# Banded attention: products with the values in float32r with split operands for two heads at a time, while the residual waits in DRAM

## The chip, the core and the metric

The kernel runs on one core of a Trainium2 chip. TensorE (PE in the rows, PEld for its weight loads), VectorE (DVE), ScalarE (ACT), GpSimd (POOL) and the DMA queues each work through a list of instructions of their own, in order, and wait for one another through semaphores. The metric is device time in microseconds of one execution.

## What is computed

The program is two blocks of a network on 512 tokens of width 1024: a recurrent layer and a differential attention layer with their MLPs, then a block that merges a banded attention with a state-space branch, followed by cross attention and an MLP. The change is in the banded attention of the second block: 16 query heads of 64, four key and value heads, blocks of 128 queries that see their own block of keys and its two neighbours, ALiBi, and a sink in the denominator.

```python
def windowed_gqa_sink(q, k, v, sink):
    ...
    s = jnp.einsum('bnqgrd,bnkgd->bngrqk', qb, kw).astype(jnp.float32) * (d ** -0.5) + bias[None]
    sink_f = sink.astype(jnp.float32).reshape(1, 1, kvh, r, 1, 1)
    m = jnp.maximum(jnp.max(s, axis=-1, keepdims=True), sink_f)
    p = jnp.exp(s - m)
    denom = jnp.sum(p, axis=-1, keepdims=True) + jnp.exp(sink_f - m)
    o = jnp.einsum('bngrqk,bnkgd->bnqgrd', (p / denom).astype(v.dtype), vw)
...
    merged = (jax.nn.sigmoid(gate_a) * (attn @ w_attn_branch[i])
              + jax.nn.sigmoid(gate_b) * (ssd @ w_ssd_branch[i]))
    x = x + merged @ w_out[i]
```

## The kernel before

Everything is float32 in value. A large product is made of three float32r products of split operands (`mm3`, lines 457 to 459): an operand is a high half, rounded to float32r by ScalarE, and a low half, the rest, subtracted by VectorE (`split`, lines 465 and 466). Weights come by SP's DMA queue into three `raw` buffers and are split into six `hl` buffers (lines 165 and 167). `feat` gives a projection with features on partitions, `tok` and `tok2` with tokens on partitions; they use the three PSUM buffers `psm`, the attention the five buffers `pss`.

The stage goes through 16 heads `hq`. A projection `gq` (two tiles of `feat`) gives the queries of four heads, so four of them; after heads 3 and 11 `gate_b` makes four tiles of another (`gb`). For a head, `Head.weights(n)` takes query block n: two float32r products over all 128 rows (query and its rest lie in one operand, keys and their rests in `k_hl`) give the scores of two or three key blocks, 256 or 384 columns (line 1476); one VectorE instruction adds the ALiBi term `A` and takes the minimum (1479; scores carry a minus sign); ScalarE takes the exponential with its sum (1481). After block 3 the sink's exponential (1484), the sum (1485) and the reciprocal (1486) follow. `Head.values(n)` multiplies the weights `e` by the reciprocal on VectorE (1494), transposes them on TensorE (1497), copies them out of PSUM on ScalarE (1499) and multiplies with the values in float32, 64 columns of stationary values against 128 queries (1501). Both heads of a pair write into one PSUM bank, which is split into `uk(i)` when the second is done.

The loop calls `values(n)` of head `hq - 2` ahead of `weights(n)` of head `hq`. Behind the stage come the tiles of `ga`, copied into `ta` (1533), which lies in the place of `A`, `e` and `PT` (`wk.phase()`). No hand orders the engines' lists: the framework's scheduler takes instructions in about program order, and what is ready earlier moves ahead, so the projections lie between the heads' steps as far as the buffers let them.

`h` holds the residual. The state-space branch before uses its place, so it waits in DRAM (`hD`, line 1169) and is loaded on GpSimd's queue before this stage (1432); it is next added to by the products with `w_out`, behind the stage.

```python
        if hq < 16:
            heads.append(Head(hq))
        for n in range(4):
            if hq >= 2:
                heads[hq - 2].values(n)
            if hq < 16:
                heads[hq].weights(n)
```

Of the kernel before, what the change touches and what calls it, by code (L numbers as in the profile page):

```python
# [18 lines left out]
P = 128  # L19
S = 512  # L20
D = 1024
NT = 4
# [224 lines left out]
def body(ctx, tc, I, out, dbg=None, stop=None):  # L247
    nc = tc.nc
# [14 lines left out]
    def PS():  # L263
        return ps_s.tile([P, 512], F32, tag="s", name="pss")
# [96 lines left out]
    WT = Weights(nc, raw_p, spl_p, specs, 6, 3)  # L361
# [4 lines left out]
    h = fix.tile([P, NT, D], F32, name="h")  # L366
# [14 lines left out]
    ident = const.tile([P, P], F32, name="ident")  # L381
# [22 lines left out]
    ps = PS()  # L404
# [12 lines left out]
    st = {}  # L417
# [11 lines left out]
    def open_wk(rounded=0):  # L429

        if "wctx" in st:
            st["wctx"].close()
        st["wctx"] = ExitStack()
        wp = st["wctx"].enter_context(tc.tile_pool(name="wp", bufs=1))
        n = 8384 - rounded
        st["wk"] = Work(wp.tile([P, n], F32, name="WK"), n)
        if rounded:
            r = wp.tile([P, rounded], F32R, name="WR")
            return [r[:, i:i + 512] for i in range(0, rounded, 512)]

    def close_b():
# [5 lines left out]
    def uk(k):  # L447
        if k < 4:
            return UAh[:, k], UAl[:, k]
        return st["UBh"][:, k - 4], st["UBl"][:, k - 4]  # L450
# [10 lines left out]
    def split(dst, src, scale=None):  # L461

        hi, lo = dst
        if scale is None:
            nc.scalar.activation(out=hi, in_=src, func=AF.Copy)  # L465
            nc.vector.tensor_tensor(out=lo, in0=src, in1=hi.bitcast(F32), op=ALU.subtract)  # L466
        else:
            nc.scalar.activation(out=hi, in_=src, func=AF.Copy, scale=scale)  # L468
            nc.vector.scalar_tensor_tensor(out=lo, in0=src, scalar=scale, in1=hi.bitcast(F32), op0=ALU.mult, op1=ALU.subtract)
# [115 lines left out]
    def tok(w, src, evac, n_k=8, tiles=NT):  # L585

        for t in range(0, tiles, 2):
            ps = PM()
            for j in range(2):
                o = ps[:, j * 256:(j + 1) * 256]  # L590
                tk = slice((t + j) * P, (t + j + 1) * P)
                for k in range(n_k):
                    xh, xl = src(k)
                    mm3(o, (xh[:, tk], xl[:, tk]), w[k], k == 0, k == n_k - 1)
            evac(slice(t, t + 2), ps.rearrange("p (a b) -> p a b", a=2))
# [164 lines left out]
    o = 0  # L760
# [6 lines left out]
    ps = PS()  # L767
    nc.tensor.transpose(ps[:, :n_rows], ROWS, ident[:n_rows, :n_rows])
    nc.scalar.activation(out=COL, in_=ps[:, :n_rows], func=AF.Copy)
    y = st["ev"].tile([P, D], F32, tag="y", name="y")  # L770
# [496 lines left out]
    class Group:  # L1267


        def __init__(s, g):  # L1270
            s.g, s.hs = g, 4 * g
# [157 lines left out]
        G[g].third()  # L1429
    ssd_out_group(7)  # L1430
    for t in range(NT):
        nc.gpsimd.dma_start(h[:, t], hD[t * P:(t + 1) * P, :])
    for t in range(NT):
        dump("ssd", acc[:, t], t)
    st["ctx"].close()
    open_b()
# [2 lines left out]
        return  # L1439


    KP = open_wk(4096)
    wk = st["wk"]
    k_hl = [KP[0:4], KP[4:8]]

    def gk_evac(n, ps):

# [5 lines left out]
                nc.vector.tensor_tensor(out=kl[r1], in0=ps[r], in1=kh[r].bitcast(F32), op=ALU.subtract)  # L1453

    feat(WT.get("gk"), xk, gk_evac)
    v = st["GP"].rearrange("p (t n) -> p t n", t=NT)
    tok(WT.get("gv"), xk, lambda t, ps: nc.scalar.activation(out=v[:, t], in_=ps, func=AF.Copy))
    pos = {}

    class Head:  # L1460
        def __init__(s, hq):
            s.hq, s.i, s.p, s.kv = hq, hq // 2, hq % 2, hq // 4
            s.A = wk.get("A", 384, 2)
            nc.vector.tensor_scalar(out=s.A, in0=band, scalar1=float(2.0 ** (-0.5 * (hq + 1))), scalar2=None, op0=ALU.mult)
            s.mn = sm.tile([P, 16], F32, tag="mg", name="mg")
            s.es = []

        def weights(s, n):

            hq, mn = s.hq, s.mn  # L1470
            lo, hi = max(0, n - 1), min(4, n + 2)
            wd = (hi - lo) * P
            bo = (lo - n + 1) * P
            ps = PS()
            for x in range(2):
                nc.tensor.matmul(ps[:, :wd], uk(s.i)[s.p][:, n * P:(n + 1) * P], k_hl[x][s.kv][:, lo * P:hi * P],  # L1476
                                 start=x == 0, stop=x == 1)
            e = wk.get(f"e{wd}", wd, 4)
            nc.vector.tensor_tensor_reduce(out=e, in0=ps[:, :wd], in1=s.A[:, bo:bo + wd], scale=1.0,
                                           scalar=nsink[:, hq:hq + 1], op0=ALU.add, op1=ALU.min, accum_out=mn[:, n:n + 1])  # L1480
            nc.scalar.activation(out=e, in_=e, func=AF.Exp, scale=-1.0, bias=mn[:, n:n + 1], accum_out=mn[:, 4 + n:5 + n])
            s.es.append((e, lo, hi))
            if n == 3:
                nc.scalar.activation(out=mn[:, 8:12], in_=mn[:, 0:4], func=AF.Exp, bias=sink[:, hq:hq + 1])
                nc.vector.tensor_tensor(out=mn[:, 8:12], in0=mn[:, 8:12], in1=mn[:, 4:8], op=ALU.add)
                nc.vector.reciprocal(out=mn[:, 12:16], in_=mn[:, 8:12])

        def values(s, n):
            if s.p == 0 and n == 0:
                pos[s.i] = PS()  # L1490
            po, r0 = pos[s.i], slice(64 * s.p, 64 * s.p + 64)
            e, lo, hi = s.es[n]
            wd = (hi - lo) * P
            nc.vector.tensor_scalar(out=e, in0=e, scalar1=s.mn[:, 12 + n:13 + n], scalar2=None, op0=ALU.mult)
            pt = PS()
            for j in range(hi - lo):
                nc.tensor.transpose(pt[:, j * P:(j + 1) * P], e[:, j * P:(j + 1) * P], ident)  # L1497
            PT = wk.get("PT", 384, 2)
            nc.scalar.activation(out=PT[:, :wd], in_=pt[:, :wd], func=AF.Copy)
            for j in range(hi - lo):  # L1500
                nc.tensor.matmul(po[r0, n * P:(n + 1) * P], v[:, lo + j, s.kv * 64:(s.kv + 1) * 64], PT[:, j * P:(j + 1) * P],  # L1501
                                 start=j == 0, stop=j == hi - lo - 1)
            if s.p == 1 and n == 3:
                split(uk(s.i), po)

    def gate_b(u):
        def gb_evac(t, ps):
# [4 lines left out]

        tok2(WT.get(f"gb{u}"), xk, gb_evac)

    heads = []
    for hq in range(18):
        u = hq // 4
        if hq % 4 == 0 and u < 4:
            feat(WT.get(f"gq{u}"), xk, lambda n, ps: split_q(2 * u + n, ps))
        if hq < 16:  # L1520
            heads.append(Head(hq))
        for n in range(4):
            if hq >= 2:
                heads[hq - 2].values(n)
            if hq < 16:
                heads[hq].weights(n)
        if hq % 8 == 3 and hq < 16:
            gate_b(u)
    wk.phase()
    ta = wk.get("ta", 4096).rearrange("p (t n) -> p t n", t=NT)  # L1530
    for u in range(2):
        tok2(WT.get(f"ga{u}"), xk,
             lambda t, ps: nc.scalar.activation(out=ta[:, t, u * 512:(u + 1) * 512], in_=ps, func=AF.Tanh, scale=0.5))
# [165 lines left out]
```

## Time and profile before

| | |
|---|---|
| median of 3 runs | 2580.79 us (2578.79 to 2582.44) |
| profiled execution, its own time | 2581.83 us |
| its span | 2580.1 us |
| PE, PEld busy | 2504.9 us (97%), 2088.2 us (81%) |
| DVE, ACT, POOL busy | 1714.5, 1220.2, 183.5 us |
| mean granted clock of TensorE | 0.989 |

The span is the time from the first to the last instruction; the rest of an execution's time lies around it. A matmul's length in a row is from its start to the modelled end of its pipeline, so neighbours overlap: what one costs TensorE is read from start to start. An fp32 product stands as two rows. The granted clock is 1.00 at 2.4 GHz and 0.50 at 1.2 GHz.

### The profile page before, as it was taken

What the parts mean: (1) busy time and instruction counts of PE and PEld (TensorE: products, weight loads), DVE (VectorE), ACT (ScalarE), POOL (GpSimd) and SP (SyncE); (2) the same over time, 40 slices, a digit from 0 to 9 for tenths busy, and PEclk for the clock granted to TensorE, in tenths of its full rate; (3) what the DMA queues carried; (4) which work ended last, traced back from release to release, by engine and by line L of the source; (5) the groups of instructions that cost most, each with busy time, mean ns of one, the idle gap of its engine ahead of it and who ended that gap; (6) DMA issues with size and microseconds to landing.
All of it is one profiled execution on the core that took longest, in us unless ns stands there. A gap on an engine that the chain in (4) does not pass through costs nothing. (4 is left out here: it accounts for less than half of the span.)

```text
span 2580.1 us, 33650 instructions
## 1 busy us (share of the span) xinstructions
PE 2504.9 (97%) x12848; PEld 2088.2 (81%) x12848; DVE 1714.5 (66%) x3048; ACT 1220.2 (47%) x2181; POOL 183.5 (7%) x199
## 2 busy tenths in 40 slices
PE   8999999999999989999999999998999999999998
PEld 7888888778888768877888788787887789878877
DVE  5566567775566657577477788887555466487674
ACT  6333345443476554444356554563455436444342
POOL 1100220000201030000121100010000000100000
PEclk9999999999999989999999999998999999999999
DMA  5521235333232133453334333352221233243441
GB/s 175 162 66 61 87 115 169 125 108 129 82 96 89 63 97 113 140 179 98 102 109 125 106 104 109 104 148 77 73 67 40 84 113 123 82 147 104 141 139 58
DMA packets 202001, 278.11 MB, mean 108 GB/s; under 512 B 10800, under 2 KB 127776, under 8 KB 201840
## 3 DMA queue, kind: packets, MB, share of 16 engines
q1 hardware_dynamic: 190352, 236.29, 29.4%
q0 software_dynamic: 10192, 34.96, 5.0%
q10 hardware_dynamic: 1296, 4.72, 0.5%
q8 instruction: 101, 1.65, 0.3%
q14 instruction: 60, 0.49, 0.1%
HBM read 271.56 MB, written 9.61 MB: 109 GB/s over the span
## 5 line engine op out<-in xcount | busy, mean ns | idle before, releaser
L458 PE MATMUL psm<-XTl,hl 128*128 128x512 f32 (+1 forms) x1400 | 537.3, 384 | 7.8 <-DVE XTl L466 7.8
L457 PE MATMUL psm<-XTh,hl 128*128 128x512 f32 (+1 forms) x1400 | 534.5, 382 | 5.9 <-ACT XTh L465 5.1
L459 PE MATMUL psm<-XTh,hl 128*128 128x512 f32 (+1 forms) x1400 | 533.3, 382 | 0.0
L165 ACT ACTIVATE hl<-raw 128x1024 fp32r<-128x1024 f32 x303 | 319.3, 1056 | 313.9 <-PE psm L459 132.6
L167 DVE TENSOR_TENSOR hl<-raw,hl 128x1024 fp32r<-128x1024 f32 x287 | 352.7, 1233 | 149.0 <-ACT hl L165 147.9
L458 PEld LDWEIGHTS psm<-XTl,hl 128*128 128x128 f32 x1400 | 266.3, 190 | 56.9 <-DVE XTl L466 8.6
L457 PEld LDWEIGHTS psm<-XTh,hl 128*128 128x128 f32 x1400 | 265.9, 190 | 55.7 <-ACT XTh L465 6.1
L459 PEld LDWEIGHTS psm<-XTh,hl 128*128 128x128 f32 x1400 | 266.3, 190 | 48.5
L457 PE MATMUL psm<-hl,XTh 128*128 128x512 f32 (+1 forms) x640 | 231.1, 362 | 4.4 <-ACT XTh L465 3.3
L458 PE MATMUL psm<-hl,XTh 128*128 128x512 f32 (+1 forms) x640 | 229.9, 359 | 0.1
L459 PE MATMUL psm<-hl,XTl 128*128 128x512 f32 (+1 forms) x640 | 229.1, 358 | 0.0
L457 PE MATMUL psm<-hl,UAh 128*128 128x512 f32 x368 | 148.6, 405 | 4.9 <-DVE ACC L625 1.5
L458 PE MATMUL psm<-hl,UAh 128*128 128x512 f32 x368 | 144.9, 395 | 0.0
L459 PE MATMUL psm<-hl,UAl 128*128 128x512 f32 x368 | 143.7, 396 | 0.0
L457 PEld LDWEIGHTS psm<-hl,XTh 128*128 128x128 f32 x640 | 122.3, 191 | 21.8 <-ACT XTh L465 3.7
L458 PEld LDWEIGHTS psm<-hl,XTh 128*128 128x128 f32 x640 | 122.2, 191 | 16.6 <-issue 0.5
L459 PEld LDWEIGHTS psm<-hl,XTl 128*128 128x128 f32 x640 | 122.3, 191 | 15.9 <-issue 0.5
L671 ACT ACTIVATE WK<-psm 128x512 f32<-128x512 f32 x66 | 39.5, 598 | 160.8 <-PE psm L459 160.8
L457 PE MATMUL psm<-hl,UBh 128*128 128x512 f32 (+1 forms) x240 | 93.5, 391 | 1.1 <-ACT UBh L468 0.8
L459 PE MATMUL psm<-hl,UBl 128*128 128x512 f32 (+1 forms) x248 | 94.3, 388 | 0.0
L1257 DVE SCALAR_TENSOR_TENSOR WS<-psm,CW,WS 128x511 f32<-128x511 f32 (+1 forms) x120 | 87.5, 740 | 8.7 <-ACT WS L1253 8.4
L458 PE MATMUL psm<-hl,UBh 128*128 128x512 f32 (+1 forms) x240 | 92.2, 386 | 0.0
(481 smaller groups left out, 4839.2 us busy)
## 6 DMA issues: line engine op xcount, KB each, us to landing
raw<-in_mlp_w_down_dram SPq DMA_DIRECT2D x76, 512.0 KB, 3.3
raw<-in_mlp_w_up_dram SPq DMA_DIRECT2D x64, 512.0 KB, 3.9
raw<-in_w_in_dram SPq DMA_DIRECT2D x60, 512.0 KB, 3.7
raw<-in_w_down_dram SPq DMA_DIRECT2D x38, 512.0 KB, 3.9
WS<-aD POOLq DMA_DIRECT2D x32, 512.0 KB, 5.9
raw<-in_w_up_dram SPq DMA_DIRECT2D x32, 512.0 KB, 3.7
raw<-in_w_in_dram SPq DMA_DIRECT2D x33, 256.0 KB, 3.2
raw<-in_a_w_in_dram SPq DMA_DIRECT2D x16, 512.0 KB, 4.9
```

Of the source, the lines that this page charges most:

```text
L165: s.nc.scalar.activation(out=h, in_=r, func=AF.Copy)
L167: eng.tensor_tensor(out=l, in0=r, in1=h.bitcast(F32), op=ALU.subtract)
L457: nc.tensor.matmul(ps, a[0], b[0], start=first, stop=False, skip_group_check=partial)
L458: nc.tensor.matmul(ps, a[0], b[1], start=False, stop=False, skip_group_check=partial)
L459: nc.tensor.matmul(ps, a[1], b[0], start=False, stop=last, skip_group_check=partial)
L671: nc.scalar.activation(out=rl, in_=ps, func=AF.Relu)
L1257: nc.vector.scalar_tensor_tensor(out=dst[:, o0:o1], in0=ps[:, o0 + d:o1 + d], scalar=cw(j), in1=dst[:, o0:o1], op0=ALU.mult, op1=ALU.add)
```

## The change

- The stage goes through eight pairs of heads. `values(n)` of pair i - 1 is called ahead of `weights(n)` of pair i.
- The values are split (`gv_evac`): for each key block and value head, 64 columns of high and 64 of low halves lie side by side in `v_hl`, one stationary operand of 128 columns.
- The weights of both heads are transposed side by side, two key blocks (512 columns) to a chunk, and split into `PT` high and low (two buffers). A query block has one or two chunks. Each key block takes two float32r products of 256 columns, with the high and with the low half of `PT` (line 1534 of the new program).
- The output has the high half's part on 64 partitions and the low half's on the other 64, heads swapped over; a copy on ScalarE (1540) and an addition on VectorE (1541) of 64 rows by 256 columns join them into `y`, for each head after blocks 1 and 3. `y`, now in SBUF, is split into `uk(i)`.
- The multiplication with the reciprocal moves from VectorE to GpSimd (1498).
- `e` and `y` lie in the place of `h`, `A` in that of `GP`; `k_hl`, `PT` and `v_hl` fill a rounded tile `WR` of 8192 words. The load of `h` moves behind the stage. `ta` comes from a work area opened anew, whose place `WR` had.

```diff
-    for t in range(NT):
-        nc.gpsimd.dma_start(h[:, t], hD[t * P:(t + 1) * P, :])
...
-    KP = open_wk(4096)
-    wk = st["wk"]
+    KP = open_wk(8192)
+
+    hw, gw = Work(h.rearrange("p t d -> p (t d)"), 4096), Work(st["GP"], 1024)
     k_hl = [KP[0:4], KP[4:8]]
+    WR = st["WR"]
+    PTs = [WR[:, 4096 + 1024 * i:5120 + 1024 * i].rearrange("p (x n) -> p x n", x=2) for i in range(2)]
+    v_hl = WR[:, 6144:8192].rearrange("p (t k n) -> p t k n", t=NT, k=4)
...
-    tok(WT.get("gv"), xk, lambda t, ps: nc.scalar.activation(out=v[:, t], in_=ps, func=AF.Copy))
+    def gv_evac(t, ps):
+
+        hi, lo = (v_hl[:, t, :, 64 * x:64 * x + 64] for x in range(2))
+        ps = ps.rearrange("p a (k n) -> p a k n", k=4)
+        nc.scalar.activation(out=hi, in_=ps, func=AF.Copy)
+        nc.vector.tensor_tensor(out=lo, in0=ps, in1=hi.bitcast(F32), op=ALU.subtract)
+
+    tok(WT.get("gv"), xk, gv_evac)
...
+        def scale(s, n):
+            e, lo, hi = s.es[n]
+            nc.gpsimd.tensor_scalar(out=e, in0=e, scalar1=s.mn[:, 12 + n:13 + n], scalar2=None, op0=ALU.mult)
+
+    class Pair:
+
+
+        def __init__(s, i):
+            s.i, s.kv = i, i // 2
+            s.heads = [Head(2 * i), Head(2 * i + 1)]
+            s.y = hw.get("yv", 512, 2).rearrange("p (n q) -> p n q", n=4)
+
+        def weights(s, n):
+            for x in s.heads:
+                x.weights(n)
+
         def values(s, n):
...
-            nc.vector.tensor_scalar(out=e, in0=e, scalar1=s.mn[:, 12 + n:13 + n], scalar2=None, op0=ALU.mult)
-            pt = PS()
-            for j in range(hi - lo):
-                nc.tensor.transpose(pt[:, j * P:(j + 1) * P], e[:, j * P:(j + 1) * P], ident)
-            PT = wk.get("PT", 384, 2)
-            nc.scalar.activation(out=PT[:, :wd], in_=pt[:, :wd], func=AF.Copy)
-            for j in range(hi - lo):
-                nc.tensor.matmul(po[r0, n * P:(n + 1) * P], v[:, lo + j, s.kv * 64:(s.kv + 1) * 64], PT[:, j * P:(j + 1) * P],
-                                 start=j == 0, stop=j == hi - lo - 1)
-            if s.p == 1 and n == 3:
-                split(uk(s.i), po)
+            lo, hi = s.heads[0].es[n][1:]
+            for x in s.heads:
+                x.scale(n)
+            if n % 2 == 0:
+                s.po = PS()
+            o = s.po[:, n % 2 * 256:n % 2 * 256 + 256]
+            for j0 in range(lo, hi, 2):
+                js = range(j0, min(j0 + 2, hi))
+                w = 256 * len(js)
+                pt = PS()
+                for j in js:
+                    for x in s.heads:
+                        c = (j - j0) * 256 + x.p * P
+                        nc.tensor.transpose(pt[:, c:c + P], x.es[n][0][:, (j - lo) * P:(j - lo + 1) * P], ident)
+                st["pt"] = st.get("pt", 0) + 1
+                PT = PTs[st["pt"] % 2]
+                split((PT[:, 0, :w], PT[:, 1, :w]), pt[:, :w])
+                for j in js:
+                    c = slice((j - j0) * 256, (j - j0) * 256 + 256)
+                    for x in range(2):
+                        nc.tensor.matmul(o, v_hl[:, j, s.kv], PT[:, x, c], start=j == lo and x == 0, stop=j == hi - 1 and x == 1)
+            if n % 2 == 1:
+                po = s.po.rearrange("p (n x q) -> p n x q", n=2, x=2)
+                y = s.y[:, n - 1:n + 1]
+                for x in range(2):
+                    r, r1 = slice(64 * x, 64 * x + 64), slice(64 - 64 * x, 128 - 64 * x)
+                    nc.scalar.activation(out=y[r], in_=po[r1, :, x], func=AF.Copy)
+                    nc.vector.tensor_tensor(out=y[r], in0=po[r, :, x], in1=y[r], op=ALU.add)
+            if n == 3:
+                split(uk(s.i), s.y.rearrange("p n q -> p (n q)"))
...
-    for hq in range(18):
-        u = hq // 4
-        if hq % 4 == 0 and u < 4:
+    for i in range(9):
+        u = i // 2
+        if i % 2 == 0 and u < 4:
             feat(WT.get(f"gq{u}"), xk, lambda n, ps: split_q(2 * u + n, ps))
...
-            if hq >= 2:
-                heads[hq - 2].values(n)
-            if hq < 16:
-                heads[hq].weights(n)
+            if i >= 1:
+                pairs[i - 1].values(n)
+            if i < 8:
+                pairs[i].weights(n)
...
-    wk.phase()
+    open_wk(4096)
+    wk = st["wk"]
     ta = wk.get("ta", 4096).rearrange("p (t n) -> p t n", t=NT)
+    for t in range(NT):
+        nc.gpsimd.dma_start(h[:, t], hD[t * P:(t + 1) * P, :])
```

TensorE, late in the stage, before the change. L1476 are score products, L1497 transpositions, L1501 value products; `pss` is PSUM, `WR` the keys, `UB` the queries, `WK` holds `e` and the transposed weights, `GP` the values.

```order
L1476 MATMUL pss<-WR,UBh 128x256 x2
L1497 MATMUL pss<-ident,WK 128x128 x3
L1476 MATMUL pss<-WR,UBh 128x384 x2
L1497 MATMUL pss<-ident,WK 128x128 x3
L1476 MATMUL pss<-WR,UBh 128x384 x2
L1501 MATMUL pss<-WK,GP 64x128 x3
L1497 MATMUL pss<-ident,WK 128x128 x2
L1476 MATMUL pss<-WR,UBh 128x256 x2
L1501 MATMUL pss<-WK,GP 64x128 x3
L1497 MATMUL pss<-ident,WK 128x128 x2
```

Transpositions and value products are those of head `hq - 2`, score products those of head `hq`; a whole head lies between a head's last score products and its first transposition.

TensorE at the same place after the change: L1484 are score products, L1527 transpositions (out of `h`, where `e` lies), L1534 value products (`WR` holds values and `PT`).

```order
L1527 MATMUL pss<-ident,h 128x128 x4
L1534 MATMUL pss<-WR 128x256
L1484 MATMUL pss<-WR,UBh 128x256 x2
L1484 MATMUL pss<-WR,UBl 128x256 x2
L1534 MATMUL pss<-WR 128x256 x4
L1527 MATMUL pss<-ident,h 128x128 x4
L1534 MATMUL pss<-WR 128x256
L1484 MATMUL pss<-WR,UBh 128x256 x2
L1484 MATMUL pss<-WR,UBl 128x256 x2
L1527 MATMUL pss<-ident,h 128x128 x4
```

The two rows of 256-column score products in the middle are the last of pair p + 1; four value products of pair p's block 3 follow, then the first four transpositions of pair p + 1 itself. From there to the end of the stage no projection stands in the list; behind its last value products the products of `ga` go on.

GpSimd after the change, the eight multiplies of one pair; the number behind `mg` tells the head. Before, GpSimd's list has nothing in this stage.

```order
L1498 TENSOR_SCALAR h_78<-h_78,mg_14366 128x256
L1498 TENSOR_SCALAR h_78<-h_78,mg_14366 128x384 x2
L1498 TENSOR_SCALAR h_78<-h_78,mg_14366 128x256
L1498 TENSOR_SCALAR h_78<-h_78,mg_14368 128x256
L1498 TENSOR_SCALAR h_78<-h_78,mg_14368 128x384 x2
L1498 TENSOR_SCALAR h_78<-h_78,mg_14368 128x256
```

All four blocks of a pair's first head stand ahead of the second head's.

## Rows read from the trace of the kernel before

**Rows 1.** Windows: length; PE, PEld, DVE, ACT, POOL busy (instructions); PEclk; DMA share; GB/s.

```profile
1841.00:1976.70 135.70, 135.70 (x729) 109.68 (x727) 75.31 (x190) 69.90 (x164) 0.00 (x0) 1.00 0.21 63
1976.70:2013.20 36.50, 35.97 (x245) 26.98 (x244) 24.03 (x89) 26.85 (x84) 0.00 (x0) 1.00 0.01 1
2013.20:2036.30 23.10, 23.09 (x117) 17.50 (x117) 6.09 (x8) 9.28 (x15) 0.00 (x0) 1.00 0.29 92
```

**Rows 2.** Groups by line, 1841 to 2036 us: busy us, mean ns | idle before.

```profile
L1501 PE MATMUL pss<-WK,GP 128*64 128x128 f32 x319 | 43.5, 281 | 0.0
...
L1479 DVE CUSTOM_DVE_ANT_0 WK<-pss,WK,nsink 128x384 f32<-128x384 f32 x32 | 19.6, 616 | 19.9 <-PE pss L1476 19.7
L1481 ACT ACTIVATE WK<-WK,mg 128x384 f32<-128x384 f32 x32 | 19.6, 612 | 8.3 <-DVE mg L1479 8.2
...
L1481 ACT ACTIVATE WK<-WK,mg 128x256 f32<-128x256 f32 x32 | 16.0, 501 | 1.9 <-DVE mg L1479 1.8
L1479 DVE CUSTOM_DVE_ANT_0 WK<-pss,WK,nsink 128x256 f32<-128x256 f32 x32 | 15.4, 480 | 18.9 <-PE pss L1476 18.8
...
L1494 DVE TENSOR_SCALAR WK<-WK,mg 128x384 f32<-128x384 f32 x32 | 11.9, 415 | 0.0
L1494 DVE TENSOR_SCALAR WK<-WK,mg 128x256 f32<-128x256 f32 x32 | 11.2, 350 | 0.4
...
L1464 DVE TENSOR_SCALAR WK<-band 128x384 f32<-128x384 f32 x14 | 5.0, 359 | 0.4
...
L466 DVE TENSOR_TENSOR UAl<-pss,UAh 128x512 fp32r<-128x512 f32 x4 | 2.8, 692 | 3.7 <-ACT UAh L465 3.6
...
L465 ACT ACTIVATE UAh<-pss 128x512 fp32r<-128x512 f32 x4 | 2.4, 598 | 5.3 <-PE pss L1501 5.3
```

**Rows 3.** Timeline from 1932.2 us: start, length, engine, line, instructions.

```profile
1932.23 0.30 PEld L1476 LDWEIGHTS pss<-WR,UAl 128*128 128x128 f32 x2
1932.25 0.49 PE L1476 MATMUL pss<-WR,UAl 128*128 128x256 f32 x2
1932.47 0.35 PEld L1497 LDWEIGHTS pss<-ident,WK 128*128 128x128 f32 x3
1932.58 0.49 PE L1497 MATMUL pss<-ident,WK 128*128 128x128 f32 x3
...
1932.80 0.30 PEld L1476 LDWEIGHTS pss<-WR,UAl 128*128 128x128 f32 x2
1932.80 0.47 DVE L1479 CUSTOM_DVE_ANT_0 WK<-pss,WK,nsink 128x256 f32<-128x256 f32 x1
...
1933.16 0.49 ACT L1499 ACTIVATE WK<-pss 128x384 f32<-128x384 f32 x1 [0.18 <-PE pss L1497]
```

**Rows 4.** Timeline: the last steps of a head's weights.

```profile
1928.92 0.16 DVE L1485 TENSOR_TENSOR mg<-mg 128x4 f32<-128x4 f32 x1
1929.12 0.18 DVE L1486 RECIPROCAL mg<-mg 128x4 f32<-128x4 f32 x1
```

**Rows 5.** A subtraction of 256 columns out of PSUM (line 1382).

```profile
L1382 DVE TENSOR_TENSOR WS<-pss,WS x32: 402/416/425, 1405.5 to 1787.3; 128x256 f32<-128x256 f32 x32
```

**Rows 6.** GpSimd's groups by line, whole span.

```profile
L634 POOL TENSOR_TENSOR WK<-ACC,GP 128x512 f32<-128x512 f32 x32 | 43.6, 1376 | 362.5 <-DVE ACC L625 349.0 <-DVE h L637 12.4 <-DVE rr L484 1.0
L167 POOL TENSOR_TENSOR hl<-raw,hl 128x1024 fp32r<-128x1024 f32 x16 | 41.9, 2636 | 411.5 <-ACT hl L165 411.5
```

**Rows 7.** Timeline of TensorE: two idle times before 1782.5 and 1790.7 us.

```profile
1782.52 1.97 PE L1381 MATMUL pss<-WS 128*128 128x64 f32 x8 [2.42 <-DVE WS L1382]
...
1790.67 1.94 PE L1394 MATMUL pss<-ident,h 128*128 128x128 f32 x8 [3.35 <-DVE h L1392]
```

**Rows 8.** Windows at half the clock.

```profile
1782.00:1790.60 8.60, 3.94 (x16) 3.56 (x16) 5.90 (x19) 1.93 (x8) 1.01 (x1) 0.50 0.13 50
...
1793.10:1799.00 5.90, 5.83 (x14) 4.58 (x15) 1.41 (x2) 0.60 (x2) 0.35 (x1) 0.50 0.54 181
```

**Rows 9.** Additions into the residual `h` after the stage (line 625).

```profile
L625 DVE TENSOR_TENSOR h<-psm,h x16: 673/688/692, 2098.2 to 2144.2; 128x512 f32<-128x512 f32 x16
```

More of the change, by code (lines that the diff above doesn't have):

```diff
@@ L437, in open_wk @@
         if rounded:
-            r = wp.tile([P, rounded], F32R, name="WR")
+            r = st["WR"] = wp.tile([P, rounded], F32R, name="WR")
             return [r[:, i:i + 512] for i in range(0, rounded, 512)]
@@ L1455, in body @@
     feat(WT.get("gk"), xk, gk_evac)
-    v = st["GP"].rearrange("p (t n) -> p t n", t=NT)
-    tok(WT.get("gv"), xk, lambda t, ps: nc.scalar.activation(out=v[:, t], in_=ps, func=AF.Copy))
-    pos = {}
+    def gv_evac(t, ps):
[4 more added lines that the diff above has]
+    tok(WT.get("gv"), xk, gv_evac)
     class Head:
@@ L1462, in __init__ @@
             s.hq, s.i, s.p, s.kv = hq, hq // 2, hq % 2, hq // 4
-            s.A = wk.get("A", 384, 2)
+            s.A = gw.get("A", 384, 2)
             nc.vector.tensor_scalar(out=s.A, in0=band, scalar1=float(2.0 ** (-0.5 * (hq + 1))), scalar2=None, op0=ALU.mult)
@@ L1477, in weights @@
                                  start=x == 0, stop=x == 1)
-            e = wk.get(f"e{wd}", wd, 4)
+            e = hw.get(f"e{wd}", wd, 4)
             nc.vector.tensor_tensor_reduce(out=e, in0=ps[:, :wd], in1=s.A[:, bo:bo + wd], scale=1.0,
@@ L1486, in weights @@
                 nc.vector.reciprocal(out=mn[:, 12:16], in_=mn[:, 8:12])
-        def values(s, n):
[L1489 to L1493, printed above, removed]
-            nc.vector.tensor_scalar(out=e, in0=e, scalar1=s.mn[:, 12 + n:13 + n], scalar2=None, op0=ALU.mult)
-            pt = PS()
-            for j in range(hi - lo):
-                nc.tensor.transpose(pt[:, j * P:(j + 1) * P], e[:, j * P:(j + 1) * P], ident)
-            PT = wk.get("PT", 384, 2)
-            nc.scalar.activation(out=PT[:, :wd], in_=pt[:, :wd], func=AF.Copy)
-            for j in range(hi - lo):
-                nc.tensor.matmul(po[r0, n * P:(n + 1) * P], v[:, lo + j, s.kv * 64:(s.kv + 1) * 64], PT[:, j * P:(j + 1) * P],
-                                 start=j == 0, stop=j == hi - lo - 1)
-            if s.p == 1 and n == 3:
-                split(uk(s.i), po)
+        def scale(s, n):
+            e, lo, hi = s.es[n]
+            nc.gpsimd.tensor_scalar(out=e, in0=e, scalar1=s.mn[:, 12 + n:13 + n], scalar2=None, op0=ALU.mult)
@@ L1513, in gate_b @@
         tok2(WT.get(f"gb{u}"), xk, gb_evac)
-    heads = []
-    for hq in range(18):
-        u = hq // 4
-        if hq % 4 == 0 and u < 4:
+    pairs = []
+    for i in range(9):
+        u = i // 2
+        if i % 2 == 0 and u < 4:
             feat(WT.get(f"gq{u}"), xk, lambda n, ps: split_q(2 * u + n, ps))
-        if hq < 16:
-            heads.append(Head(hq))
+        if i < 8:
+            pairs.append(Pair(i))
         for n in range(4):
-            if hq >= 2:
-                heads[hq - 2].values(n)
-            if hq < 16:
-                heads[hq].weights(n)
-        if hq % 8 == 3 and hq < 16:
+            if i >= 1:
+                pairs[i - 1].values(n)
+            if i < 8:
+                pairs[i].weights(n)
+        if i % 4 == 1 and i < 8:
             gate_b(u)
-    wk.phase()
+    open_wk(4096)
+    wk = st["wk"]
     ta = wk.get("ta", 4096).rearrange("p (t n) -> p t n", t=NT)
+    for t in range(NT):
+        nc.gpsimd.dma_start(h[:, t], hD[t * P:(t + 1) * P, :])
     for u in range(2):
```

## Prediction

> **What bounds the kernel now.** Read first the windows of the stage. From the first score product to the last value product it takes 195.3 us in three stretches [rows 1]: 135.7 us with projections between the attention's products, 36.5 us without any, 23.1 us with products of gate `ga` between the last heads'. See that TensorE is busy for all of each at full clock, while DVE is busy 105.4 us and ACT 106.0 us in the sum. So here TensorE's work is the time, and latency costs nothing. Then read the groups by line: the 160 fp32 products with the values (two trace rows each) hold TensorE 43.5 us [rows 2], 0.272 us each with the entry and exit of their bursts. Then read the timeline for what a float32r product of 256 columns takes: two issue in 1932.23 to 1932.47, 0.12 us each; three transpositions in 1932.47 to 1932.80, 0.11 each [rows 3].
>
> **The change part by part.** *Value products.* 160 fp32 products of 0.272 us become 160 float32r ones (8 pairs x 10 blocks x 2 halves), 256 columns wide, at 0.12. With latency hidden that is 160 x 0.152 = 24.3 us less. Bounds of the new price: 0.12 [rows 3] and, if they issued no faster than now, 0.272 [rows 2]. I take 0.12, the row with type and width in common.
>
> *Where they stand* (counted in TensorE's list of instructions). Projections are the only work that can fill TensorE's waits, and the same 406 products stand in the first stretch before and after; but before they accompany 78 of the 160 value products, 82 of the 160 transpositions and 74 score products, now 44, 50 and 54. A pair now holds `e` from its scores to its values with no head between, and the list runs out of projections earlier. So:
>
> - First stretch: less 78 x 0.272 = 21.2, less 32 x 0.11 = 3.5, less 10 score products of 256 columns at 0.12 and 10 of 384 at an estimated 0.18 (1.5 times as wide) = 3.0, plus 44 x 0.12 = 5.3: 135.7 - 22.4 = 113.3 us. TensorE stays the bound there, since DVE's 75 and ACT's 70 us [rows 1] leave room.
> - Third stretch: the 18 value products (4.9) and 10 transpositions (1.1) leave, 23.1 - 6.0 = 17.1; its copies into `ta` now wait until everything in `WR` is done, and three tiles of `ga` hold all `psm` buffers till then. One copy of 512 columns (0.60 [rows 2]), the half result ahead of it on ACT and hand-overs: 1.2. Together 18.3 us.
> - Second stretch: 116 value products, 110 transpositions and 74 score products, and no projection. TensorE's part is small: a pair takes 20 x 0.11 + 20 x 0.12 + 8 x 0.12 + 8 x 0.18 = 7.0 us. The time is the loop from pair to pair.
>
> *The loop, first half,* from the last score products of pair p+1 to its first transposition. Score product to DVE 0.55 (1932.25 to 1932.80 [rows 3]); two reductions of 256, 0.96 [rows 2]; then on DVE, ahead of the sums, the low half of pair p's last chunk 0.69 and two `A` tiles 0.72 [rows 2]; sum 0.16 and reciprocal 0.18 [rows 4]: 3.3 us. Then POOL: it has all four multiplies of head 0 ahead of head 1's, and the second transposition is head 1's, so five multiplies (three of 256, two of 384) stand in the way. Before, values ran two heads behind scores and this lay under the head between.
>
> *Price of a multiply on GpSimd.* The trace has none with one input. Lower bound: DVE's own 0.350 and 0.415 [rows 2], 1.9 us for the five. Upper: GpSimd's two-input rows, 1376 ns for 512 and 2636 for 1024 columns [rows 6], that is 0.116 + 2.46 ns a column, 0.75 and 1.06: 4.4 us. I take the middle, 3.1, since one input is less than two but the engine is GpSimd. With 0.2 of hand-overs the first half is 6.6 us.
>
> The Trainium skill, GPSIMD Engine Reference, Engine selection, calls one-input elementwise work on GpSimd "roughly line-rate" and sends elementwise tiles to VectorE. By its rate the price would lie at the lower bound and the sum 7 us lower; no run here shows it yet.
>
> *Second half,* from there to the next last score products, a zigzag in which each engine's list makes it wait for the other: four transpositions to ACT 0.7 (0.58 for three [rows 3], one more 0.11), high half 0.60, low half 0.69, reduction 256 0.48, two exponentials 1.00, high half 0.60, low halves 0.69 and 0.42, reduction 384 0.62, two exponentials 1.22, high half 0.60, low half 0.69, sum of the halves 0.42, reduction 384 0.62, low half 0.42, last products 0.3 [rows 2, 5]: 10.1 us. (256-column subtractions and the 64-row sum are priced by line 1382.)
>
> So 16.7 us a pair, with TensorE at work for 7.0. The stretch holds the rest of pair 2 (half of the zigzag and one first half, 11.7), four full loops (66.8) and pair 7's values without scores, six chunks of high and low half, about 8: 86.5 us in place of 36.5.
>
> *Clock.* TensorE idles over 3 us in every first half. In the trace it was granted 0.50 (1.2 of 2.4 GHz) from 1782 on, after idle times of 2.42 and 3.35 us [rows 7], through sparse work and through 5.9 us of dense products at the end [rows 8]. Half rate adds between 1.5 us (transpositions, score and last products that lie on the loop) and 7.0 us (all its work) to a pair. Weighing it as present about half the time, nearer the lower end, I take 1.2 a pair, 7 us in all, and nothing for the restart.
>
> *Edits at nothing.* The `h` load: four issues leave POOL at 1792, where nothing follows, and come behind the last multiply; the first use was at 2098.2 [rows 9], 62 us behind the stage. The `mem` load on POOL, now ahead of pair 7's multiplies, waits only for the last reductions, which these wait for too. Two low halves of the values (0.69 each) lie under projections. SP's list is unchanged.
>
> *Sum.* 113.3 + 86.5 + 18.3 = 218.1, plus 7 = 225 for 195.3: 29.8 more. The profiled execution took 2581.83, so 2611.6 there; it lies 1.0 above the median of the runs, 2580.79. **Forecast: 2611 us.**
>
> The Trainium skill, SBUF — State Buffer, has VectorE operations with two SBUF inputs and GpSimd operations lock each other out of a shared port pair. The split of a finished pair (inputs now both in SBUF) falls among the multiplies; by the rule it would add at most one 0.69 a pair, 4 us.
>
> **Rivals.**
> - *The loop overlaps better than the lists say* and only DVE's own time counts in the second stretch: per pair 6.0 us for values (four low halves of 0.69, two of 0.42, four sums of 0.42, the pair's split 0.69) and 5.8 for scores (four reductions of 0.48, four of 0.62, 0.72 for `A`, 0.68 for sums and reciprocals). 5.8 pairs of values (116 of 20) and 4.6 of scores (74 of 16) make 61.5: 113.3 + 61.5 + 18.3 = 193.1, 2.2 under before: 2579 us, not slower. It decides below a loop of 11.0 us, where the second stretch comes to 63.7. For it: DVE and ACT were busy only 24 and 27 of 36.5 us [rows 1]. Against it: each step above waits for a result.
> - *TensorE stays the bound throughout:* 24.3 us less, 2556. It needs projections in the second stretch, and the list has none.
> - *Half clock throughout:* 4 us a pair and 3 at the restart, 26 in place of 7: 2630. For it the long idle times; against it, dense runs of several us in each loop.
> - *Cheap multiplies at full clock:* 1.2 a pair less, no clock term: 2598; with a loop of 14 us, 2589.
>
> **How the numbers follow.** Forecast 0.65 (2598 to 2622), half clock 0.15, cheap and short 0.12, DVE's time 0.05, TensorE's bound 0.03. The range 2590 to 2632 leaves out the last two and the tails. A measurement tells 0.2%, 5.2 us, from no change. Slower: the first three, 0.92. DVE's time, 2.2 us, falls within: same 0.05. TensorE's bound alone is faster: 0.03.
>
> **What would show it.** Windows: first stretch near 113 us with TensorE full; then 85 to 95 us with TensorE under half busy and one wait for POOL per pair of over 3 us. Groups: float32r products without bursts' gaps, multiplies on POOL of 0.4 to 1.0 us. PEclk at half for part of the second stretch. Wrong: a second stretch under 64 us, or TensorE full in it; multiplies outside their bounds; time moved outside the stage.

## Result and profile after the change

| | before | after |
|---|---|---|
| median of 4 runs each, same chip | 2581.61 us (2578.79 to 2582.87) | 2616.94 us (2616.21 to 2618.18) |
| profiled execution, its own time | 2581.83 us | 2618.18 us |
| its span | 2580.1 us | 2616.1 us |
| PE, PEld busy | 2504.9, 2088.2 us | 2498.3, 2092.0 us |
| DVE, ACT, POOL busy | 1714.5, 1220.2, 183.5 us | 1735.8, 1233.0, 258.8 us |
| mean granted clock | 0.989 | 0.978 |

The ratio is 1.0139 (95% interval 1.0121 to 1.0156): slower, 36 us by the spans. The first addition into `h` behind the stage came at 2098.2 us before [rows 9] and comes at 2134.6 now, 36.4 later; the first score product comes at 1843.2 for 1841.3. So the loss lies in the stage: it takes 34.3 us more. Of the other 2 us, 1.6 are there at the first product of line 1381, long ahead of the changed code: 1401.9 us before, 1403.5 here. It starts at 1405.5 in e4_before_scale_gpsimd, which differs from the kernel before only later, so this is scatter between executions.

```profile
L625 DVE TENSOR_TENSOR h<-psm,h x16: 672/688/692, 2134.6 to 2180.6; 128x512 f32<-128x512 f32 x16
```

Windows of the kernel after, with the columns of [rows 1]. The first boundary is where the projections run out and 44 value products are done, as counted in the prediction; the second is the last value product; the third row holds the 70 products of `ga` that stood inside the stage before.

```profile
1843.18:1955.00 111.82, 111.82 (x557) 94.70 (x556) 63.62 (x133) 57.02 (x121) 30.07 (x24) 1.00 0.26 76
1955.00:2055.50 100.50, 58.30 (x300) 48.90 (x298) 55.52 (x164) 52.67 (x146) 46.34 (x44) 0.75 0.04 14
2055.50:2072.80 17.30, 16.21 (x72) 13.27 (x72) 6.17 (x7) 8.20 (x12) 0.53 (x1) 1.00 0.60 198
```

To be read against [rows 1]: TensorE full in the first stretch, 58% busy in the second, where the granted clock is 0.75 and no engine comes near its length. For whom TensorE waited in the second stretch (1955 to 2056 us; engine line waited for: us in total, times, longest us):

```profile
PE pss L1527 <- POOL h L1498: 26.9, 10, 4.4
PE pss L1534 <- ACT WR L465: 9.5, 12, 1.4
PE pss L1534 <- DVE WR L466: 5.4, 6, 1.1
```

The same view of the whole stage before has 0.5 us in all. One loop of the second stretch, from the timeline (start, length, engine, line, instructions, [idle before]):

```profile
1981.35 0.18 DVE L1494 RECIPROCAL mg<-mg 128x4 f32<-128x4 f32 x1
...
1981.72 9.02 POOL L1498 TENSOR_SCALAR h<-h,mg 128x256 f32<-128x256 f32 x8 [10.23 <-DVE mg L1493]
...
1982.70 0.33 PE L1527 MATMUL pss<-ident,h 128*128 128x128 f32 x1 [1.31 <-POOL h L1498]
...
1987.45 0.90 PE L1527 MATMUL pss<-ident,h 128*128 128x128 f32 x3 [4.42 <-POOL h L1498]
1988.45 0.60 ACT L465 ACTIVATE WR<-pss 128x512 fp32r<-128x512 f32 x1 [4.66 <-PE pss L1527]
1989.08 0.69 DVE L466 TENSOR_TENSOR WR<-pss,WR 128x512 fp32r<-128x512 f32 x1 [4.51 <-ACT WR L465]
...
1998.54 0.45 PE L1484 MATMUL pss<-WR,UBl 128*128 128x256 f32 x2
...
2001.14 0.18 DVE L1494 RECIPROCAL mg<-mg 128x4 f32<-128x4 f32 x1
...
2001.51 0.92 POOL L1498 TENSOR_SCALAR h<-h,mg 128x256 f32<-128x256 f32 x1 [10.77 <-DVE mg L1493]
```

GpSimd starts its eight multiplies 0.2 us behind the end of the first head's reciprocal (shown; the second head's starts 0.28 later). The second head's first transposition waits until 1987.45, five multiplies and 5.73 us later, and ScalarE and VectorE stand idle for over 4.5 us behind it. The zigzag (the blocks in which TensorE, ScalarE and VectorE wait for each other in turn) to the pair's last scores takes 1987.45 to 1998.54, sums and reciprocals 2.97 more, and the next multiplies start at 2001.51.

What a multiply and a value product take (groups by line of the stage, columns of [rows 2]):

```profile
L1498 POOL TENSOR_SCALAR h<-h,mg 128x384 f32<-128x384 f32 x32 | 42.8, 1346 | 0.0
L1534 PE MATMUL pss<-WR 128*128 128x256 f32 x160 | 40.3, 339 | 15.3 <-ACT WR L465 9.5 <-DVE WR L466 5.4
...
L1498 POOL TENSOR_SCALAR h<-h,mg 128x256 f32<-128x256 f32 x32 | 32.0, 1004 | 172.2 <-ACT mg L1492 80.2 <-DVE mg L1494 31.8 <-DVE mg L1493 31.6
```

From start to start a value product takes 0.120 us where the granted clock is 1.00 (median of 128) and 0.214 where it is 0.50 (median of 32), against 0.272 before. Five of them at half the clock, 1993.53 to 1994.60:

```profile
1993.53 1.27 PE L1534 MATMUL pss<-WR 128*128 128x256 f32 x5
1994.60 0.68 PE L1527 MATMUL pss<-ident,h 128*128 128x128 f32 x4
```

### The profile page after: what moved, and what is told of

It reads as the page before. It is cut to its first block, busy times and chain, and to the rows that moved or that the text cites. A ratio compares the mean times of both kernels' runs of the same rounds, so it can differ in the third digit from the quotient of the medians.

```text
span 2616.1 us, 33503 instructions
## 1 busy us (share of the span) xinstructions
PE 2498.3 (95%) x12688; PEld 2092.0 (80%) x12688; DVE 1735.8 (66%) x3066; ACT 1233.0 (47%) x2197; POOL 258.8 (10%) x263
## 5 line engine op out<-in xcount | busy, mean ns | idle before, releaser
L458 PEld LDWEIGHTS psm<-hl,XTh 128*128 128x128 f32 x640 | 121.8, 190 | 17.3 <-DVE hl L172 1.2
```

The source lines that it names most:

```text
L458: nc.tensor.matmul(ps, a[0], b[1], start=False, stop=False, skip_group_check=partial)
```

## Experiments

Theory A is the prediction's: results from pair to pair set the second stretch, since nothing lies between a pair's last scores and its first transposition. Each kernel was timed against the kernel before on its own chip; the medians of before were 2582.2 to 2583.4 us.

**Multiplies on VectorE (e1_scale_vector).**

```diff
-            nc.gpsimd.tensor_scalar(out=e, in0=e, scalar1=s.mn[:, 12 + n:13 + n], ...)
+            nc.vector.tensor_scalar(out=e, in0=e, scalar1=s.mn[:, 12 + n:13 + n], ...)
```

> The changed kernel with the eight multiplies of a pair back on VectorE, nothing else undone. Theory A (the loop from pair to pair in the second stretch is the time, and the five multiplies on GpSimd, 5.7 us of its 19.4, stand in it uncovered): the first half shrinks to about 2.3 us (three of 0.35, two of 0.42, one sum of halves between), VectorE's list gives back some 0.5, so about 3 us a pair over four to five pairs: 2600 to 2606 us. Theory B (the zigzag of the second half and VectorE's own time set the loop, the multiplies only fill a wait that is there anyway): VectorE gets 3.1 us a pair more, and the time stays at 2613 or rises.

**Multiplies on GpSimd, in the order of use (e2_scale_order).** The four numbers of both heads lie in one tile `mm`.

```diff
...
-                nc.vector.reciprocal(out=mn[:, 12:16], in_=mn[:, 8:12])
+                if s.p == 1:
...
+                    nc.vector.reciprocal(out=mm[:, :, 12:16], in_=mm[:, :, 8:12])
```

> The changed kernel with the multiplies still on GpSimd, but sum and reciprocal of both heads in one instruction each, so that the two multiplies of block 0 come first and each block's pair in the order of use. Theory A: the first transposition of the second head waits for two multiplies (1.84 us) in place of five (5.7), and the other six lie under the blocks ahead of them: about 3.5 us a pair less, 2598 to 2604 us. Theory B (GpSimd's 8.6 us a pair are too much wherever they stand, or the zigzag is the bound): every block waits for its own two multiplies, 2612 or more.

Measured: 2598.7 us on VectorE (1.0060, 1.0043 to 1.0077) and 2605.4 in order (1.0085, 1.0070 to 1.0100), 18 and 11.5 us under the changed kernel; both are 1.3 to 1.4 us outside theory A's ranges, the first below, the second above, and more than 6 us from theory B's. Windows of one loop each: of the changed kernel, from the first multiply of one pair to that of the next,

```profile
1981.72:2001.51 19.79, 11.50 (x56) 9.89 (x56) 10.78 (x34) 10.38 (x30) 9.02 (x8) 0.74 0.00 1
```

with the multiplies in order, from reciprocal to reciprocal,

```profile
1994.12:2010.10 15.98, 11.32 (x56) 9.25 (x56) 10.62 (x32) 10.36 (x30) 9.01 (x8) 0.79 0.00 1
```

and with the multiplies on VectorE.

```profile
1977.53:1992.43 14.90, 10.34 (x57) 8.72 (x56) 12.79 (x42) 10.14 (x29) 0.00 (x0) 0.89 0.01 2
```

The loop loses 3.8 and 4.9 us (from pair to pair the loops take 18.8 to 19.8 us in the changed kernel, 15.7 to 16.4 in order, 14.9 to 15.7 on VectorE). The clock of these windows rises from 0.74 to 0.79 and 0.89; what share of the gain is the clock's was not told apart. Theory B falls: VectorE takes 2 us more a loop, and the loop is shorter. GpSimd is as busy in the second row as in the first (9.0 us); only what stands ahead of the transpositions changed. With the multiplies away from GpSimd about half of the 35 us is gone; the other half, 16.5 us over the kernel before, does not come from GpSimd. Multiplies still stand in the loop there, on VectorE: TensorE waits 11.1 us in all for them.

**The kernel before, with no head between (e3_before_no_head_between).**

```diff
-    for hq in range(18):
+    for hq in range(17):
...
-            if hq >= 2:
-                heads[hq - 2].values(n)
+            if hq >= 1:
+                heads[hq - 1].values(n)
```

> The kernel before with one edit: the values run one head behind the weights in place of two, still in fp32, single heads, multiplies on VectorE. Theory A (what the change lost is the work between a pair's last scores and its first transposition): the first half of a head, about 1.9 us, and the steps of the blocks stand open in some eight heads without projections, 60 us in place of 37: 2592 to 2610 us. Theory C (TensorE's list and its projections cover this in the kernel before in any case; the loss is in GpSimd and in pairs with split halves): 2578 to 2585 us.

**The kernel before, multiplies on GpSimd (e4_before_scale_gpsimd).**

```diff
-            nc.vector.tensor_scalar(out=e, in0=e, scalar1=s.mn[:, 12 + n:13 + n], ...)
+            nc.gpsimd.tensor_scalar(out=e, in0=e, scalar1=s.mn[:, 12 + n:13 + n], ...)
```

> The kernel before with one edit: the four multiplies of a head on GpSimd (about 4.3 us a head). Theory A (a slow multiply costs nothing as long as a whole head of 4.6 to 7 us lies between): 2578 to 2587 us. Theory D (GpSimd's price counts wherever it stands): each of the some six heads of the second stretch gets 2 to 3 us longer, 2592 us or more.

Measured: 2604.9 us without the head between (1.0083, 1.0068 to 1.0098), 2584.8 with GpSimd's multiplies (1.0005, 0.9995 to 1.0014: no difference that can be told). Windows of the kernel without the head between, up to where its projections run out and from there to the products of `ga`:

```profile
1842.50:1969.30 126.80, 126.80 (x645) 101.81 (x643) 63.34 (x145) 59.75 (x129) 0.00 (x0) 1.00 0.23 67
1969.30:2036.50 67.20, 53.02 (x338) 41.45 (x336) 37.60 (x131) 38.34 (x119) 0.00 (x0) 0.92 0.00 1
```

Taking the head away costs the kernel before 23 us, with no float32r value products, no pairs and nothing on GpSimd: its second stretch shows TensorE idle for 14 of 67 us and a clock of 0.92. Multiplies of GpSimd's price, 74.4 us of them in all, cost nothing that can be told where that head is left: no wait of TensorE for one stands in that trace. Theories C and D fall. It is not the slow multiply that costs, but a slow multiply with nothing beside it. No run takes the steps that the change adds to the zigzag (the split of `PT`, the joining of the halves) out alone, so their share stays open.

**Projections spread.** Three kernels spread the tiles of `gq` and `gb` over the loops: alone (e5_spread_projections), with the multiplies in order (e6_spread_and_order), with the multiplies on VectorE (e7_spread_and_vector).

```diff
-                s.po = PS()
+                s.po = PM()
...
+            if (i, n) in FILL:
+                fill(*FILL[i, n])
```

> The changed kernel, multiplies on GpSimd as they are, with the same projections spread: one tile (24 products, about 5.1 us) after blocks 1 and 3 of each pair where there is one left, held there by letting the output banks of the values take their place in psm between them. Theory A (what is missing is other work for TensorE while the loop waits): each of seven loops holds about 7 us of attention and 10 us of projections under a loop of 16 to 17.5 us at full clock, the half clock goes, the stage takes 165 to 190 us for 213: 2568 to 2592 us. Theory E (the loop of results itself is the time; tiles put into TensorE's list in order only lie in its path): 2605 us or more, with every loop over 20 us.

> The projections spread as in e5_spread_projections, and the multiplies on GpSimd in the order of use as in e2_scale_order. Theory A: the loop without its 3.4 us of multiplies lies near 13 to 16 us, so that TensorE's 17 us of work a pair are the bound: 5 to 15 us under e5_spread_projections, 2556 to 2575 us, under both kernels. Theory E: no better than 2600.

> The projections spread as in e5_spread_projections, and the multiplies on VectorE as in e1_scale_vector. Theory A: as e6_spread_and_order, 2554 to 2575 us; VectorE has 24.5 us more to do in the stage, in all some 150 of 170, so that it may come out some us above e6. Theory E: no better than 2600.

Measured: 2612.8, 2602.4 and 2591.6 us, 3 to 7 us under the same kernels with the tiles early, and 17 to 27 over the upper ends of theory A; the first two came out as theory E has it (from one pair's multiplies to the next 21 to 30 us in the first), the third lies between the two theories. The edit also moves the output banks of the values from the five buffers `pss` to the three `psm`, and no run has that alone. TensorE and GpSimd in the first of them, from the timeline:

```profile
1902.72 0.40 PE L459 MATMUL psm<-hl,XTl 128*128 128x512 f32 x1
1902.95 0.28 PE L1534 MATMUL psm<-WR 128*128 128x256 f32 x1
1905.11 0.62 PE L1534 MATMUL psm<-WR 128*128 128x256 f32 x3 [1.88 <-DVE WR L466]
1908.66 0.47 PE L1527 MATMUL pss<-ident,h 128*128 128x128 f32 x1 [2.92 <-POOL h L1498]
```

```profile
1907.68 8.69 POOL L1498 TENSOR_SCALAR h<-h,mg 128x256 f32<-128x256 f32 x8 [20.20 <-DVE mg L1493]
```

The tile's last product (line 459) ends just ahead of the idle time: the tile stands in front of the wait, not in it. An in-order list is fixed ahead of the run; a product that could run during a wait does so only if it stands behind the last scores and ahead of the first transposition.

**Tiles tied into the wait.** A tile is written over the bank of its pair's last score product, so that it cannot start ahead of it; once with the multiplies on VectorE (e8_fill_in_wait_vector), once in order on GpSimd (e9_fill_in_wait_order).

```diff
-                fill(*FILL[i, n])
+                fill(*FILL[i, n], pairs[i].heads[1].ps if n == 3 else None)
```

> As e7_spread_and_vector, but one tile of each pair is tied to the end of its scores: it is written over the bank of the pair's last score product, so that it cannot start ahead of it and stands in TensorE's list between the last scores and the first transposition, where the loop waits; the others come after block 1. Theory F (in e5 to e7 the list put the tiles ahead of the wait in place of into it, since the wait is only known on the chip): TensorE's 20 us of idle time in the stage of e7 shrink to under 10, its half clock goes: 2570 to 2584 us. Theory G (VectorE, busy 7 to 7.8 of 8 us in several stretches of e7, is the bound by then): 2587 to 2595 us, with TensorE's waits moved to VectorE's results.

> As e6_spread_and_order, with the tiles tied as in e8_fill_in_wait_vector and the multiplies on GpSimd in the order of use. Theory F: a tile of 5.1 us covers the multiplies ahead of the first transposition (1.84 us) and two more, VectorE has 24 us less to do than in e8: 2562 to 2580 us. Theory G: 2585 or more; as GpSimd's multiplies and VectorE's splits of weights (two inputs in SBUF, 1.23 us each) hold each other, part of the gain is lost: 1 us a multiply that meets one.

Measured: 2593.6 and 2591.0 us: no gain on VectorE, 11 us on GpSimd, where the waits for multiplies went down from 11.1 us in the stage (e6_spread_and_order) to 2.1. What is left is told by the view of waits of that kernel:

```profile
PE pss L457 <- DVE GP L1487: 6.8, 6, 3.1
PE psm L1537 <- DVE WR L466: 4.9, 6, 1.7
PE pss L1530 <- POOL h L1500: 2.1, 2, 1.7
```

The first row is the price of the tie: the tile waits for the reduction that frees the bank. Theory F fails: both times lie above its ranges, and TensorE's idle time, which was to fall from 20 us to under 10, stayed, as the stages of e7_spread_and_vector and e8_fill_in_wait_vector show (180.65 us with TensorE busy for 160.91, 180.24 with 160.54); on GpSimd it fell from 22.6 us to 18.8. The tile covers the wait for the multiplies, and another wait takes its place.

```profile
1841.73:2022.38 180.65, 160.91 (x828) 134.91 (x827) 132.69 (x360) 107.00 (x267) 2.19 (x4) 0.93 0.19 59
1841.42:2021.66 180.24, 160.54 (x831) 133.23 (x830) 132.96 (x360) 107.68 (x267) 2.20 (x4) 0.96 0.19 59
```

Theory G's times are the ones that came out. That VectorE is the bound is not shown for the stage as a whole: it is busy for 7.6 and 7.9 of 8 us, with TensorE at 5.1, in stretches of e7_spread_and_vector, and for 7.9 with TensorE at 5.8 in one of e9_fill_in_wait_order, but for 133 of 181 us and 115 of 182 of their stages.

**Half a pair between (e10_half_pair_between).**

```diff
-            e = hw.get(f"e{wd}", wd, 4)
+            e = hw.get(f"e{wd}", wd, 8 if wd == 256 else 4)
...
+        for n in (1, 2, 0, 3):
+            pairs[i].values(n)
+            j = i + (1 if n in (1, 2) else 2)
+            if j < 8:
+                pairs[j].weights(n)
```

> The changed kernel with half a pair put back between a pair's last scores and its first transposition, in the same memory (four more 256-column places for e, one less for y): blocks in the order 1, 2, 0, 3, and the scores of blocks 0 and 3 a pair further ahead, so that values 0 and 3 of pair i and scores 0 and 3 of pair i + 2 lie under the sums and multiplies of pair i + 1. Multiplies on GpSimd in the order of use as in e2_scale_order, projections left to the list as in the changed kernel; two more tiles A a pair (0.7 us on VectorE). Theory A (the cover is the point): the 1.84 us of multiplies and some 2 us of sums ahead of them, open in e2's loop of 16.1, lie under two blocks: a loop of 12 to 13.5 us, 2588 to 2598 us. Theory G (VectorE's list, 12.5 us of work a pair, and the zigzag set the loop): no gain on e2_scale_order, 2603 us or more.

Measured: 2585.2 us (1.0009, 1.0000 to 1.0019), level with the kernel before and 32 under the changed one: 11.5 of that is the order of the multiplies (e2_scale_order), the other 20 came with the half pair between. Windows of this kernel: the full stretch, the rest to the last value product; then two loops of it.

```profile
1842.10:1961.00 118.90, 118.90 (x612) 101.65 (x611) 75.23 (x168) 66.87 (x152) 38.51 (x32) 1.00 0.24 72
1961.00:2023.30 62.30, 47.53 (x245) 37.70 (x243) 46.17 (x129) 41.82 (x116) 37.38 (x36) 0.86 0.06 19
```

```profile
1967.97:1982.23 14.26, 9.89 (x60) 7.62 (x59) 11.60 (x36) 10.50 (x31) 8.72 (x8) 1.00 0.01 2
1982.23:1996.47 14.24, 11.51 (x55) 9.46 (x56) 10.80 (x33) 9.76 (x29) 9.10 (x8) 0.76 0.00 1
```

GpSimd works 9.1 us in the loop as in the changed kernel, and TensorE waits 1.7 us in all for it. Two of its loops, 14.3 and 14.2, are longer than the 12 to 13.5 I expected (a third takes 12.6), yet the time is under my range. One reason is that the covered pairs get further while projections still run: 612 instructions of TensorE by 1961.0 (587 by 1960.6 in the changed kernel); it is 62 us from there to the last value product in place of 95. The two loops shown also have clocks of 1.00 and 0.76 at one and the same length, so a lower clock need not make a loop longer.

**Half a pair between, projections spread.** Twice (e11_half_pair_and_spread, e12_half_pair_spread_early), the tiles dealt out in two ways.

> As e10_half_pair_between, with the projections spread tile by tile as in e5 to e7 (output banks of the values in psm). Theory A: the loop of 12 to 13.5 us lies under 17 us of work that TensorE has a pair, so that TensorE is nearly full at full clock and the 24 us of the cheaper products show: 2560 to 2578 us, under both kernels. Theory G: VectorE, in some 145 us of work of the stage's 175, still lets TensorE wait a third of the time it waits in e9: 2580 to 2590 us.

> As e11_half_pair_and_spread with the tiles dealt out otherwise: one of gb0 and one of gq1 between the first scores (where e11 left TensorE idle for 5 us near 1852), each gq tile half a loop earlier (in e11 scores waited 4.1 us for the split of their queries), one tile in each half of the loops 0 to 4. Theory A: the 20 us that TensorE still idles in the stage in e11 fall by 8 to 12 and some of the half clock with them: 2576 to 2584 us, level with the kernel before or a little under it. Theory G (every tile in TensorE's list delays results that VectorE and ScalarE wait for, so that idle time only moves): 2588 to 2595 us, no better than e11 and worse than e10, where the tiles all come early.

Measured: 2593.1 us the first way, above the ranges of both theories and worse than with the tiles early: TensorE idled for 5 us in the first loop, and scores waited 4.1 us for the splits of queries whose tile came too late. The second way 2579.6 us (0.9987, 0.9978 to 0.9996; medians 2579.6 and 2582.5), inside theory A's range: a little under the kernel before, by less than the 0.2% I call telling, and 37 us under the changed kernel. In one and the same window, TensorE works 191.71 us at a clock of 0.89 in the changed kernel,

```profile
1841.00:2076.00 235.00, 191.71 (x950) 161.29 (x949) 126.54 (x304) 119.07 (x281) 76.95 (x69) 0.89 0.18 57
```

and in this last one more, at a higher clock:

```profile
1841.00:2076.00 235.00, 221.61 (x1110) 184.15 (x1109) 146.96 (x331) 127.60 (x291) 78.18 (x69) 0.97 0.24 74
```

The kernel before is busy for 234.46 of it at 1.00:

```profile
1841.00:2076.00 235.00, 234.46 (x1261) 186.90 (x1260) 128.23 (x314) 116.92 (x274) 0.53 (x1) 1.00 0.22 66
```

So of the 24 us that the products save, nearly all still goes into idle time and clock.

## Why the prediction was right

Forecast 2611 us, measured 2616.9, inside the range and on the side forecast. The mechanism held: TensorE stays the bound while projections last, then the loop from pair to pair is the time. Not all of its sizes did, and three of its own signs failed: the second stretch took 100.5 us for 85 to 95, TensorE was 58% busy in it and not under half, and the multiplies lie outside their bounds, which the prediction had named as a sign of being wrong. That the total is only 6 us off is in part luck: the second stretch came out 7.0 us over its forecast, the first and the third 2.5 under theirs, and 2 us more lie ahead of the changed code. Step by step, for the profiled execution:

- *First stretch:* 113.3 forecast, 111.8 measured, TensorE full. The 0.12 us of a float32r product, and so the 24.3 us of the value products, stood at full clock. *Third:* 18.3 forecast, 17.3 measured.
- *Second stretch:* 86.5 and 7 for the clock forecast, 100.5 measured. It is a loop from pair to pair as described: 18.8 to 19.8 us from one pair's multiplies to the next for the forecast 16.7 and 1.2.
- *The term that was mis-sized* is "Price of a multiply on GpSimd", of which it says "I take the middle, 3.1". Undisturbed, the five multiplies ahead of the second transposition take 5.2 us (1962.97 to 1968.20), above the upper bound of 4.4; from start to start one takes 0.90 us for 256 and 1.22 for 384 columns. The bound came from rows of 512 and 1024 columns [rows 6], drawn as a line down to 256; the multiply's 0.32 us for 128 columns is 2.5 ns a column, the slope of the two-input rows, but its length has a constant of 0.28 us and not 0.116. "One input is less than two" did not hold. In three of the five pairs a disturbance added 0.5 (below), so that the wait was 5.73.
- *First half:* 6.6 forecast, 7.8 to 8.7 measured (last score products 1998.54, transposition 2007.24), of it 2.97 ahead of the multiplies for 3.3. *Second half:* 10.1 and 1.2 forecast, 10.6 to 11.1 measured. Zigzag and clock together came out; their shares were not told apart.
- *Clock:* in every loop one half at 0.50 and one at 1.00, as weighed, not throughout. Windows of two loops of the changed kernel:

```profile
1984.50:1994.70 10.20, 6.50 (x27) 6.10 (x28) 3.79 (x12) 3.27 (x10) 6.24 (x6) 0.50 0.01 2
1994.80:2001.50 6.70, 4.57 (x29) 3.55 (x28) 5.37 (x19) 5.89 (x18) 0.00 (x0) 1.00 0.00 0
2001.70:2011.70 10.00, 4.19 (x17) 3.50 (x18) 3.13 (x8) 2.73 (x8) 8.83 (x8) 0.50 0.00 0
2011.90:2022.00 10.10, 6.28 (x40) 5.01 (x38) 7.98 (x26) 7.65 (x23) 0.89 (x1) 1.00 0.00 1
```

  It is at half from 1984.5 and from 2001.7 on, 2.8 and 0.2 us behind the first multiply of a pair, in which TensorE has little to do, and back at full in the zigzag.
- *Edits at nothing:* the later load of `h` cost nothing that shows: behind the stage the distance to before stays at 36 us to the end.
- *Rivals:* VectorE's time as the bound needed a loop under 11 us; even on its best footing, half a pair between, the loop is 12.6 to 14.3. Cheap multiplies fell by their price, half clock throughout by the rows above. That the list has no projection in the second stretch was the condition of TensorE's bound; when they were put there it still did not become the bound.

The Trainium skill, GPSIMD Engine Reference, Engine selection, calls one-input work on GpSimd "roughly line-rate". The trace does not agree: a multiply takes 0.92 us for 256 and 1.24 for 384 columns against VectorE's 0.350 and 0.415 [rows 2], 2.6 and 3.0 times as long.

## What to carry to other kernels

Before an edit that shortens work on the full engine, see what that work covers: a list with a whole head between producer and consumer hides the sums, the reciprocals and the multiplies between them, and an edit that takes the head away pays for all of them at once. Price an engine's instruction from rows of its own kind and width, and take the constant with the slope. Work meant to fill a wait must stand in the in-order list between the two instructions that wait, which is where a schedule made ahead of the run need not put it.

## What the runs showed of the hardware

In the changed kernel a multiply on GpSimd takes the same to within some 30 ns each time (0.92 or 1.24 us), unless a VectorE instruction whose two inputs both lie in SBUF is under way as it starts, or starts with it. Durations of the five multiplies 1981.7 to 1987.0 us, of two widths (ns min/median/max), in the changed kernel:

```profile
L1498 POOL TENSOR_SCALAR h<-h,mg x5: 919/926/1750, 1981.7 to 1986.5; 128x256 f32<-128x256 f32 x3, 128x384 f32<-128x384 f32 x2
```

The five that start from 1985.6 on, the last two of them beside a subtraction out of PSUM (0.69 us from 1989.08) and a reduction out of PSUM:

```profile
L1498 POOL TENSOR_SCALAR h<-h,mg x5: 918/920/1242, 1985.6 to 1989.8; 128x256 f32<-128x256 f32 x3, 128x384 f32<-128x384 f32 x2
```

The 1750 ns are the 384-column multiply that began at 1983.84, 0.01 us behind the split of a finished pair (`UAl<-h,UAh`, 0.74 us from 1983.83): 0.51 more than its like. In the first stretch, where VectorE also splits weights (1.23 us, both inputs in SBUF), single multiplies took up to 2277 ns. It also goes the other way: the same split took 0.95 us, for 0.69, where it began at 1965.26 us, inside a multiply that ran from 1965.10 on and kept its 1.24. But it ended at 1966.21, ahead of that multiply, and where it began 0.43 us into a multiply of the same width (2042.88, the multiply from 2042.45 on) neither took longer:

```profile
1965.26 0.95 DVE L466 TENSOR_TENSOR UAl<-h,UAh 128x512 fp32r<-128x512 f32 x1 [0.70 <-ACT UAh L465]
...
2042.88 0.69 DVE L466 TENSOR_TENSOR UBl<-h,UBh 128x512 fp32r<-128x512 f32 x1 [0.70 <-ACT UBh L465]
```

Two inputs in SBUF are not the only case. In e10_half_pair_between VectorE's multiply that makes a tile `A`, with one input, took 0.65 us from 1969.16 on, for 0.35, and the multiply on GpSimd that started at 1969.57 took 0.22 more than its like.

The Trainium skill, SBUF — State Buffer, Who interferes with whom, has a VectorE operation with two SBUF inputs and a GpSimd operation lock each other out. The trace agrees that they hold each other up, and the 0.5 us in three of the pairs lies inside the 0.69 that the prediction gave as its most. It does not agree that the hold lasts to the end of the operation that came first: the split of 1965.26 was over before the multiply that it met.
